# An output projection as four pairs in seven half-size products, with its weight sums made earlier in the kernel

## The chip, the cores and the metric

The kernel runs on one core of one Trainium2 chip. The time is device microseconds (us) of one launch. The kernel before was timed three times: 1026.96, 1028.63 and 1029.95 us, median 1028.63. One execution was also profiled; its own time was 1028.81 us. The engines have short names throughout: PE multiplies matrices (PEld is its weight load), DVE is the vector engine, ACT the scalar engine, POOL the GpSimd engine, SP the one that issues most transfers.

## The reference

One decoder layer on 512 tokens of 1024 channels, float32. Two mixers run on the normed input: gated linear recurrence (RG-LRU) and sparse attention with sixteen heads. They are merged by two gates, the merged result goes through an output projection back to the residual stream, and a gated feed-forward block with a short convolution follows.

```python
merged = sigmoid(h @ w_mgr) * (rnn @ w_ro) + sigmoid(h @ w_mga) * (att @ w_ao)
x = x + merged @ w_out                    # 1024 x 1024: what the change is about
h2 = rms_norm(x, g2)
u = causal_dwconv(h2 @ w_up)              # 1024 x 6144, in 24 pairs of column blocks
y = x + (gelu(u[:, :3072]) * u[:, 3072:]) @ w_down
```

(Names are shortened; the layer's remaining parts lie ahead of these lines.)

## The kernel before

Everything is kept transposed: 128 channels on the partitions, the 512 tokens along the free axis. A projection takes a block of 128 output channels, and for each of its eight input blocks k three products (`mm3`, lines 204 to 206): high half of the weight by high half of the input, high by low, low by high. So an output block costs 24 matmuls of 512 columns. The high half of a weight, `whi`, is a cast on ACT (line 167); the low half, `wlo`, is a subtraction on DVE (line 175), or under the attention heads on POOL, in four pieces (line 172). `whi` and `wlo` have three buffers each, the raw weight `wraw` two.

The stages in order: first norm and key compression; sixteen heads, between whose steps units of other projections ("fills", three matmuls each) are put by `FILL_RATE` and `FILL_MORE`; attention output and recurrence; the merge; the output projection `w_out`; the second norm with the first up-projection; the feed-forward block; the down-projection.

The merge runs a list of steps, `MERGE`. For each output block m, `roa` is 24 matmuls, `a` six, `b` two (line 1158). `rob` prepares weights that two blocks share. Behind `b`, DVE multiplies by the gate (1159), adds the attention part (1160), and the block is split into `mh` (ACT, line 229) and `ml` (DVE, line 230). `w_out` then takes eight blocks with `mm3`, adds the residual (1172), and prepares the second norm: `xh`, `xl`, the squares, and a chain that makes the tokens' scale factors (1184 to 1198).

The last 18 of the 24 feed-forward pairs are already in another form. A pair is two output blocks of 128 channels; with the inputs' eight blocks cut into two halves and the tokens into two halves, it is a 2 by 2 block product, and seven half-size products replace eight. Each is four k by three matmuls of 256 columns (`prod`, 1305 to 1307): 84 per pair. `seed` does four of the seven (weights u1 and u2) and combines them (1323 to 1327), `rest` does the other three (weights u3 and u4). Of a pair's weights three are sums of weights. `sums` makes these ahead of time in DRAM: SP writes the first terms (1214), then POOL issues three accumulating transfers in turn (1217), each of which must wait for the one before. When a set's steps are issued is told by `SUM_AT` and `SUM_RATE`, as a function of the position in the list of weights.

```python
if n < len(js): first(js[n], h)                      # SP, two halves
add(js[n - 1], slice(0, 64), a["wa"][js[n - 1]])      # POOL, then
add(js[n - 2], slice(96, 128), self.ws[js[n - 2]][32:64])
add(js[n - 3], slice(64, 96), self.ws[js[n - 3]][96:128])
```

In most stages the order on each engine comes from a scheduler with priorities; from the first up-projection on, PE's order is that of the code (`manual_schedule`).

## Time and profile before

| what | value |
|---|---|
| median of three runs | 1028.63 us |
| profiled execution: its time, its span | 1028.81 us, 1027.0 us |
| busy: PE, DVE, ACT, POOL | 1014.5, 750.3, 614.2, 250.7 us |
| heads (85 to 355 us): PE, DVE, POOL busy of 270.00 | 267.27, 223.43, 105.37 us |
| merge (545 to 605 us): PE, DVE busy of 60.00 | 59.21, 40.70 us |
| output projection (605.00 to 648.30): PE, DVE busy of 43.30 | 43.30, 22.40 us |
| feed-forward pairs in half-size products (715 to 892): PE busy | 37.64 of 38.00, then 139.00 of 139.00 us |

The span is the time between the first and the last instruction of one execution; the 1.81 us between it and the execution's time lie outside what the profile shows. A stage's own row tells more than the shares of the whole span: where PE's busy time is as long as the stretch, the stage ends when its matmuls are issued, and where it is shorter, the difference is PE's waiting.

### The profile page before, as it was taken

To read this page: it belongs to the slowest core of one execution; us is meant where nothing else is said; L and a number is where in the kernel's file an instruction comes from. 1 tells how busy PE (TensorE), PEld (TensorE's weight loads), DVE (VectorE), ACT (ScalarE), POOL (GpSimd) and SP (SyncE) were. 2 spreads that over 40 slices of the span, in tenths; PEclk is the share of its full clock that TensorE was granted. 3 is DMA by queue.
4 is the path that set the end of the run, shared out by engine and by line. 5 is a ranking of instruction groups with operands and counts; after the bars stand their busy time and mean duration, and the time that the engine had idled before them with its cause. 6 is when DMAs were issued, how large, how long until landed. Compare 5 with 4: busy or idle time off the path is not lost.

```text
span 1027.0 us, 15691 instructions
## 1 busy us (share of the span) xinstructions
PE 1014.5 (99%) x5657; PEld 881.5 (86%) x5657; DVE 750.3 (73%) x1441; ACT 614.2 (60%) x1034; POOL 250.7 (24%) x324
## 2 busy tenths in 40 slices
PE   8999999999999999999999999999999999999998
PEld 6888888988888888888887888888999999988886
DVE  6778879888878787679598564599798888933333
ACT  6466777877777663478788534365566656533320
POOL 0264435334433300332332014222211111100000
PEclk9999999999999999999999999999999999999999
DMA  7434443354535567865432977657876566632312
GB/s 235 87 112 112 134 119 108 106 137 108 157 101 158 127 223 202 232 190 171 146 92 85 294 230 204 179 149 213 259 204 201 176 196 187 202 99 88 102 62 82
DMA packets 63022, 160.88 MB, mean 157 GB/s; under 512 B 16283, under 2 KB 17691, under 8 KB 60064
## 3 DMA queue, kind: packets, MB, share of 16 engines
q1 hardware_dynamic: 56896, 137.92, 41.1%
q0 software_dynamic: 5904, 21.81, 12.4%
q8 instruction: 44, 0.72, 0.3%
q14 instruction: 34, 0.28, 0.1%
q10 hardware_dynamic: 144, 0.15, 0.1%
HBM read 150.63 MB, written 44.04 MB: 190 GB/s over the span
## 4 chain that ended last, share of the span: by engine, by line
PE 80%; DVE 11%; ACT 4%; issue 2%; DMA 2%; SPq 0%; DVEq 0%; ACTq 0%
PE mm L206 16%; PE mm L205 16%; PE mm L204 16%; PE mm L1307 5%; PE mm L1305 5%; PE mm L1306 5%; PE O L899 3%; PE T L908 3%; DMA wraw<-in_w 2%; PE S L868 1%; PE v L750 1%; PE S L869 1%; DVE wlo L175 1%; ACT s L879 1%; DVE s L872 1%
## 5 line engine op out<-in xcount | busy, mean ns | idle before, releaser
L167 ACT CAST whi<-wraw 128x1024 fp32r<-128x1024 f32 (+2 forms) x202 | 202.7, 1005 | 224.9 <-PE misc L205 77.0
L175 DVE TENSOR_TENSOR wlo<-wraw,whi 128x1024 fp32r<-128x1024 f32 (+1 forms) x167 | 193.4, 1159 | 134.6 <-ACT whi L167 134.4
L204 PE MATMUL mm<-xh,whi 128*128 128x512 f32 x456 | 178.7, 392 | 0.0
L206 PE MATMUL mm<-xh,wlo 128*128 128x512 f32 x456 | 178.5, 391 | 0.0
L205 PE MATMUL mm<-xl,whi 128*128 128x512 f32 x456 | 178.2, 391 | 0.0
L172 POOL TENSOR_TENSOR wlo<-wraw,whi 128x256 fp32r<-128x256 f32 (+2 forms) x139 | 101.5, 783 | 131.9 <-ACT whi L167 118.9
L206 PEld LDWEIGHTS mm<-xh,wlo 128*128 128x128 f32 x456 | 85.6, 188 | 18.5
L204 PEld LDWEIGHTS mm<-xh,whi 128*128 128x128 f32 x456 | 85.7, 188 | 16.8
L205 PEld LDWEIGHTS mm<-xl,whi 128*128 128x128 f32 x456 | 85.7, 188 | 16.6
L879 ACT ACTIVATE s<-s,bs,rq 128x128 f32<-128x128 f32 (+3 forms) x128 | 82.5, 647 | 17.2 <-DVE bs L876 17.1
L230 DVE TENSOR_TENSOR ptl<-T,pth 128x512 fp32r<-128x512 f32 x80 | 54.9, 687 | 16.6 <-ACT pth L229 15.7
L204 PE MATMUL mm<-fh,whi 128*128 128x512 f32 x168 | 65.4, 389 | 0.0
L205 PE MATMUL mm<-fl,whi 128*128 128x512 f32 x168 | 65.4, 389 | 0.0
L206 PE MATMUL mm<-fh,wlo 128*128 128x512 f32 x168 | 65.4, 389 | 0.0
L229 ACT CAST pth<-T 128x512 fp32r<-128x512 f32 x80 | 46.2, 581 | 28.7 <-PE T L908 28.0
L872 DVE CUSTOM_DVE_ANT_0 s<-S,cc 128x128 f32<-128x128 f32 (+3 forms) x128 | 58.3, 483 | 2.2 <-PE S L869 1.9
L1217 POOL DMA_DIRECT2D ws<-ws x36 | 28.5, 791 | 117.6 <-DMA ws<-ws 45.9
L908 PE MATMUL T<-cc,s 128*128 128x128 f32 x320 | 48.5, 273 | 1.6 <-DVE ptl L230 1.0
L908 PEld LDWEIGHTS T<-cc,s 128*128 128x128 f32 x320 | 39.3, 140 | 12.0 <-DVE ptl L230 2.0
L1249 DVE SCALAR_TENSOR_TENSOR y<-mm,pp,y 128x511 f32<-128x511 f32 (+1 forms) x60 | 44.2, 741 | 0.1
L899 PE MATMUL O<-pth,v 128*128 128x512 f32 (+3 forms) x128 | 42.8, 352 | 0.3 <-ACT hsq L645 0.3
L884 DVE TENSOR_SCALAR s<-s,sm 128x256 f32<-128x256 f32 (+3 forms) x106 | 40.9, 431 | 1.0
(393 smaller groups left out, 2642.5 us busy)
## 6 DMA issues: line engine op xcount, KB each, us to landing
wraw<-in_w SPq DMA_DIRECT2D x126, 512.0 KB, 3.5
ws<-in_wi SPq DMA_DIRECT2D x36, 512.0 KB, 5.1
wraw<-ws SPq DMA_DIRECT2D x72, 256.0 KB, 3.2
wraw<-in_w SPq DMA_DIRECT2D x54, 256.0 KB, 3.3
ws<-in_wa POOLq DMA_DIRECT2D x18, 512.0 KB, 6.0
ws<-ws POOLq DMA_DIRECT2D x36, 256.0 KB, 4.6
xr<-in_x SPq DMA_DIRECT2D x16, 256.0 KB, 4.9
x<-in_x SPq DMA_DIRECT2D x8, 256.0 KB, 4.5
```

The lines of the kernel that those rows point to most:

```text
L167: self.last_hi = nc.scalar.copy(hi[:, :n], raw[:, :n])
L172: nc.gpsimd.tensor_sub(lo[:, e], raw[:, e], hi[:, e].bitcast(F32))
L175: nc.vector.tensor_sub(lo[:, :e], raw[:, :e], hi[:, :e].bitcast(F32))
L204: nc.tensor.matmul(ps, wh, xh, start=first, stop=False)
L205: nc.tensor.matmul(ps, wh, xl, start=False, stop=False)
L206: nc.tensor.matmul(ps, wl, xh, start=False, stop=last)
L230: self.nc.vector.tensor_sub(lo, src, hi.bitcast(F32))
L872: nc.vector.tensor_tensor_reduce(s[i, x], ps[:, x - xs[0]], mask, 1.0, -3e38, ALU.add, ALU.max, mx[:, x, i:i + 1])
L879: self.last_exp = nc.scalar.activation(s[t, x], s[t, x], AF.Exp, bias=bs[:, x, t:t + 1], scale=rq[:, t], accum_out=sm[:, x, t:t + 1])
L899: nc.tensor.matmul(O[:, q0:S], lhsT, r, start=first[0], stop=(last and n == len(rhs) - 1))
L908: nc.tensor.transpose(T[:, off:off + 128], s[i, x][:, 128 * j:128 * j + 128], self.ident)
L1305: nc.tensor.matmul(ps, w[0][:, c], xh, start=start and k == 0, stop=False, skip_group_check=True)
```

## The change

The eight blocks of `w_out` become four pairs, numbered 24 to 27, in the form that the feed-forward pairs have. `prod`, `seed` and `rest` move from the feed-forward function to methods that both stages call. The operands that the seven products need (`b11`, `t1`, `t2`, `t3`, `t4`, `b21`, `b22`) are built in the merge, behind each `b` step, by a new `prep`. The merge takes its output blocks in the order `MP`, so that the two blocks of one operand follow each other, and its last block in two column halves. Four more sets of weight sums are made, and the schedule of the sums is new: 15 sets are issued under the heads instead of 8, and three instead of ten are left for the stages behind the merge. The operands lie in what was the room of the first norm's `xh` and `xl`; the second norm's get a room of their own (`x2`). One fill unit more stands at the sixth step of head 14 (`FILL_MORE`), and three k of the second up-projection are put ahead of the token-scale matmuls.

```diff
-FILL_MORE = {..., (12, 1): 2}
+FILL_MORE = {..., (12, 1): 2, (14, 5): 1}
-SUM_AT, SUM_RATE = 20, ((43, 1.0), (66, 2.4), (82, 16.0), (116, 2.0), (999, 3.0))
+SUM_AT, SUM_RATE = 20, ((43, 0.5), (66, 3.0), (82, 16.0), (105, 32.0), (117, 1.5), (999, 3.0))
-MERGE = ("roa0 roa1 roa2 rob0 a0 a1 roa3 b0 b1 roa4 rob1 a2 b2 roa5 a3 b3 roa6 rob2 a4 b4 a5 b5 roa7 rob3 "
-         "a6 b6 a7 b7").split()
+MERGE = ("roa0 roa1 roa2 rob0 a0 a1 roa3 b0 b1 roa4 rob1 a2 b2 a3 b3 roa5 rob2 a4 b4 a5 b5 roa6 rob3 a6 b6 "
+         "roa7 a7 b7").split()
+MP = [4 * (m % 2) + m // 2 for m in range(8)]
+WO = "s24 s25 r24 s26 r25 s27 r26 r27".split()
...
+        def prep(k, x1, x2):
+            lo, hi = slice(0, 256), slice(256, 512)
+            v = nc.vector
+            if x2 is None:
+                op("b11", k, x1[:, lo])
+                v.tensor_sub(x1[:, lo], x1[:, lo], x1[:, hi])
+                op("t1", k, x1[:, lo])
+                return
+            t2 = mr.tile([128, 256], F32, name="mt", bufs=1)
+            t34 = mr.tile([128, S], F32, name="mtt", bufs=1)
+            v.scalar_tensor_tensor(t2, x1[:, lo], -1.0, x2[:, hi], ALU.mult, ALU.subtract)
+            op("t2", k, t2)
+            v.tensor_sub(t34[:, lo], x2[:, hi], x1[:, hi])
+            v.scalar_tensor_tensor(t34[:, hi], t2, -1.0, x2[:, lo], ALU.mult, ALU.subtract)
+            op("t3", k, t34, True)
+            op("b21", k, x2, True)
...
-                nc.vector.tensor_mul(sg[m], ps[m], sg[m])
-                nc.vector.tensor_add(sg[m], sg[m], self.ma[:, m])
-                self.split(self.mh[:, m], self.ml[:, m], sg[m])
+                for t in (slice(0, S),) if m < 7 else (slice(256, 512), slice(0, 256)):
+                    nc.vector.tensor_mul(sg[m][:, t], ps[m][:, t], sg[m][:, t])
+                    nc.vector.tensor_add(sg[m][:, t], sg[m][:, t], self.ma[:, MP[m], t])
+                prep(m // 2, sg[m - m % 2], sg[m] if m % 2 else None)
...
-        for m in range(8):
-            wt = self.w("wo", m)
-            ps = self.ps.tile([128, S], F32, name="mm", bufs=self.mmb)
-            for k in range(KO):
-                self.mm3(ps, wt, slice(128 * k, 128 * k + 128), (self.mh[:, k], self.ml[:, k]), k == 0, k == KO - 1)
+            for step in WO:
+                j = int(step[1:])
+                if step[0] == "s":
+                    part[j] = self.seed(j, 3 if j == FC else 4)
+                else:
+                    rest(j, *part.pop(j))
...
+            w2 = self.w("u2", j)
+            self.prod(d, w2, 512, "t1")
+            for ks in (range(late), range(late, 4)):
+                self.prod(c, w, 512, "t2", True, ks)
+                self.prod(e, w2, 0, "t3", False, ks)
...
         ps = [self.proj("up", 0)]
+        g = self.proj_g("up", FC)
+        for _ in range(3):
+            next(g)
...
-        js = list(range(NPL, FC))
+        js = [*range(FC, FC + 4), *range(NPL, FC)]
```

The order on the engines changes at three places. In the rows below, "waits" names the semaphores that an instruction waits for, and "x3" is a count.

PE at the end of the merge, before: the last weight product, the two matmuls of `b7`, and the first three of `w_out`.

```order
L206 MATMUL mm<-hgh,wlo 128x512
L1158 MATMUL mm<-hgh,whi 128x512
L1158 MATMUL mm<-hgb,whi 128x512
L204 MATMUL mm<-mh,whi 128x512 [waits Activation_49]
L205 MATMUL mm<-ml,whi 128x512
L206 MATMUL mm<-mh,wlo 128x512 [waits DVE_49]
```

The same place after. `mxh` and `mxl` are the high and low halves of `b11`, `t1` and `t2`; `myh` and `myl`, below, those of the other four operands.

```order
L217 MATMUL mm<-hgh,wlo 128x512
L1210 MATMUL mm<-hgh,whi 128x512
L1210 MATMUL mm<-hgb,whi 128x512
L1277 MATMUL mm<-mxh,whi 128x256 [waits Activation_49]
L1278 MATMUL mm<-mxl,whi 128x256
L1279 MATMUL mm<-mxh,wlo 128x256 [waits DVE_49]
```

And where the first pair's `seed` ends, after:

```order
L1277 MATMUL mm<-myh,whi 128x256
L1278 MATMUL mm<-myl,whi 128x256
L1279 MATMUL mm<-myh,wlo 128x256
L1277 MATMUL mm<-mxh,whi 128x256 [waits Activation_49]
L1278 MATMUL mm<-mxl,whi 128x256 [waits DVE_49]
L1279 MATMUL mm<-mxh,wlo 128x256
L1277 MATMUL mm<-myh,whi 128x256 [waits Activation_49]
L1278 MATMUL mm<-myl,whi 128x256 [waits DVE_49]
L1279 MATMUL mm<-myh,wlo 128x256
```

The matmuls are half as wide, and the last six of the first `seed` (k = 3 of `t2` and `t3`) wait for operands of the merge's last block.

DVE at the same place, before: the merge's last two blocks (`sg` is the gate's tile, `ma` the attention part).

```order
L1159 TENSOR_TENSOR sg<-mm,sg 128x512 [waits PE_49]
L1160 TENSOR_TENSOR sg<-sg,ma 128x512 [waits DVE_49]
L1159 TENSOR_TENSOR sg<-mm,sg 128x512 [waits PE_49]
L230 TENSOR_TENSOR ml<-sg,mh 128x512 [waits Activation_49]
L1160 TENSOR_TENSOR sg<-sg,ma 128x512 [waits DVE_49]
L175 TENSOR_TENSOR wlo<-wraw,whi 128x1024 [waits DMAHW1_49,Activation_49]
L230 TENSOR_TENSOR ml<-sg,mh 128x512 [waits Activation_49]
L1172 TENSOR_TENSOR xn<-mm,xr 128x512 [waits DMAHW4_49,PE_49]
```

After: from the second-last weight of the merge's end to the last operand. `mt` is `t2`; `mtt` holds `t3` and `t4`.

```order
L186 TENSOR_TENSOR wlo<-wraw,whi 128x1024 [waits DMAHW0_49,DMAHW1_49,PE_49,Activation_49]
L1213 TENSOR_TENSOR sg<-mm,sg 128x256 [waits PE_49]
L1213 TENSOR_TENSOR sg<-mm,sg 128x256
L1214 TENSOR_TENSOR sg<-sg,ma 128x256 [waits DVE_49]
L186 TENSOR_TENSOR wlo<-wraw,whi 128x1024 [waits Activation_49]
L1214 TENSOR_TENSOR sg<-sg,ma 128x256 [waits DVE_49]
L1175 SCALAR_TENSOR_TENSOR mt<-sg 128x256 [waits DVE_49]
L1177 TENSOR_TENSOR mtt<-sg 128x256
L1178 SCALAR_TENSOR_TENSOR mtt<-mt,sg 128x256 [waits DVE_49]
L241 TENSOR_TENSOR myl<-sg,myh 128x2x256 [waits Activation_49]
L241 TENSOR_TENSOR mxl<-mt,mxh 128x256 [waits Activation_49]
L241 TENSOR_TENSOR myl<-mtt,myh 128x2x256 [waits Activation_49]
```

The last block's multiplication now comes in halves, and three subtractions and three low halves stand behind it, with a weight's low half between them.

DVE behind the merge's first two blocks, before: `wlo` 128x512 is the low half of the weights of `rob1`, which the step `a2` needs.

```order
L1159 TENSOR_TENSOR sg<-mm,sg 128x512 [waits DMASW5_49,PE_49,Activation_49]
L1159 TENSOR_TENSOR sg<-mm,sg 128x512 [waits PE_49,Activation_49]
L181 TENSOR_TENSOR whi<-wraw,whi 84x2x128 [waits DMAHW1_49,Activation_49]
L1160 TENSOR_TENSOR sg<-sg,ma 128x512 [waits DVE_49] x2
L175 TENSOR_TENSOR wlo<-wraw,whi 128x512
L230 TENSOR_TENSOR ml<-sg,mh 128x512 [waits DMASW7_49,DMASW0_49,Activation_49]
L230 TENSOR_TENSOR ml<-sg,mh 128x512 [waits Activation_49]
L175 TENSOR_TENSOR wlo<-wraw,whi 128x1024 [waits DMAHW3_49,Activation_49]
```

After:

```order
L1213 TENSOR_TENSOR sg<-mm,sg 128x512 [waits DMASW2_49,PE_49,Activation_49]
L1213 TENSOR_TENSOR sg<-mm,sg 128x512 [waits PE_49,Activation_49]
L192 TENSOR_TENSOR whi<-wraw,whi 84x2x128 [waits DMAHW7_49,Activation_49]
L1214 TENSOR_TENSOR sg<-sg,ma 128x512 [waits DVE_49] x2
L241 TENSOR_TENSOR mxl<-sg,mxh 128x256 [waits Activation_49]
L1177 TENSOR_TENSOR mtt<-sg 128x256 [waits DMASW5_49,DMASW6_49,DMASW4_49,DVE_49]
L1169 TENSOR_TENSOR sg<-sg 128x256 [waits DVE_49]
L241 TENSOR_TENSOR myl<-sg,myh 128x2x256 [waits Activation_49]
L241 TENSOR_TENSOR mxl<-sg,mxh 128x256 [waits Activation_49]
L1175 SCALAR_TENSOR_TENSOR mt<-sg 128x256
L186 TENSOR_TENSOR wlo<-wraw,whi 128x512
L1178 SCALAR_TENSOR_TENSOR mtt<-mt,sg 128x256 [waits DVE_49]
```

Six operations of the operands of block pair 0 and 1 now stand ahead of that `wlo`.

POOL under the heads, before. `ws_1338` and the like are the sets of sums in DRAM; a `wlo` of 128x256 is a quarter of a weight.

```order
L1217 DMA ws_1338<-ws_1338 32x2048 [waits DMAHW1_49,DMASW0_49]
L1217 DMA ws_1338<-ws_1338 32x2048 [waits DMASW1_49]
L172 TENSOR_TENSOR wlo<-wraw,whi 128x256 [waits DMAHW0_49,PE_49,Activation_49]
L172 TENSOR_TENSOR wlo<-wraw,whi 128x256 x3
L1217 DMA ws_1779<-in_wa 64x2048 [waits DMAHW4_49]
L172 TENSOR_TENSOR wlo<-wraw,whi 128x256 [waits DMAHW2_49,PE_49,Activation_49]
L172 TENSOR_TENSOR wlo<-wraw,whi 128x256 x3
L172 TENSOR_TENSOR wlo<-wraw,whi 128x256 [waits DMAHW3_49,PE_49,Activation_49]
L172 TENSOR_TENSOR wlo<-wraw,whi 128x256 x3
```

After:

```order
L1334 DMA ws_1338<-ws_1338 32x2048 [waits DMAHW1_49,DMASW0_49]
L1334 DMA ws_1616<-in_wa 64x2048 [waits DMAHW3_49]
L1334 DMA ws_1338<-ws_1338 32x2048 [waits DMASW1_49]
L183 TENSOR_TENSOR wlo<-wraw,whi 128x256 [waits DMAHW0_49,PE_49,Activation_49]
L183 TENSOR_TENSOR wlo<-wraw,whi 128x256 x3
L1334 DMA ws_1616<-ws_1616 32x2048 [waits DMAHW4_49,DMASW2_49]
L1334 DMA ws_1616<-ws_1616 32x2048 [waits DMASW4_49]
L1334 DMA ws_1783<-in_wa 64x2048 [waits DMAHW6_49]
L183 TENSOR_TENSOR wlo<-wraw,whi 128x256 [waits DMAHW2_49,PE_49,Activation_49]
L183 TENSOR_TENSOR wlo<-wraw,whi 128x256 x3
L183 TENSOR_TENSOR wlo<-wraw,whi 128x256 [waits DMAHW5_49,PE_49,Activation_49]
L183 TENSOR_TENSOR wlo<-wraw,whi 128x256 x3
```

In the same stretch of the queue two sets begin where there was one, and their transfers stand between the weights' low halves.

## Rows read from the trace of the kernel before

**Rows 1.** The page, parts 1 and 2: busy times; PE's granted clock in 40 slices.

```profile
PE 1014.5 (99%) x5657; PEld 881.5 (86%) x5657; DVE 750.3 (73%) x1441; ACT 614.2 (60%) x1034; POOL 250.7 (24%) x324
...
PEclk9999999999999999999999999999999999999999
```

**Rows 2.** Busy time by stretch: stretch, length, PE, PEld, DVE, ACT, POOL, PEclk, DMA share, GB/s.

```profile
85.00:355.00 270.00, 267.27 (x1544) 230.61 (x1543) 223.43 (x683) 203.15 (x466) 105.37 (x141) 1.00 0.47 124
545.00:605.00 60.00, 59.21 (x261) 48.69 (x260) 40.70 (x53) 35.42 (x47) 9.06 (x10) 1.00 0.66 202
605.00:648.30 43.30, 43.30 (x193) 35.83 (x192) 22.40 (x28) 17.58 (x24) 14.48 (x11) 1.00 0.75 213
753.00:892.00 139.00, 139.00 (x1194) 139.00 (x1193) 118.89 (x174) 87.95 (x114) 18.17 (x14) 1.00 0.62 193
```

**Rows 3.** Timeline of PE, output projection's first matmul and the one behind its last (start, length).

```profile
604.85 0.40 PE L204 MATMUL mm<-mh,whi 128*128 128x512 f32 x1
...
648.40 0.39 PE L204 MATMUL mm<-xh,whi 128*128 128x512 f32 x1
```

**Rows 4.** Timeline of PE, half-size products: first, first of the next pair, behind the last.

```profile
715.12 0.28 PE L1305 MATMUL mm<-b11h,whi 128*128 128x256 f32 x1
...
720.73 0.28 PE L1305 MATMUL mm<-b11h,whi 128*128 128x256 f32 x1
...
892.16 0.40 PE L204 MATMUL mm<-fh,whi 128*128 128x512 f32 x1
```

**Rows 5.** Timeline of DVE in the half-size products: starts of operations that stand back to back.

```profile
732.10 1.22 DVE L175 TENSOR_TENSOR wlo<-wraw,whi 128x1024 fp32r<-128x1024 f32 x1
733.23 0.74 DVE L1249 SCALAR_TENSOR_TENSOR y<-mm,pp,y 128x510 f32<-128x510 f32 x1
733.89 0.74 DVE L1249 SCALAR_TENSOR_TENSOR y<-mm,npw,y 128x511 f32<-128x511 f32 x1
...
736.86 0.43 DVE L1325 TENSOR_TENSOR mm<-mm,ac 128x256 f32<-128x256 f32 x1
737.20 0.42 DVE L1326 TENSOR_TENSOR mm<-mm,ac 128x256 f32<-128x256 f32 x1
```

**Rows 6.** Timeline of DVE and PE at the merge's step a2.

```profile
574.54 1.28 DVE L1160 TENSOR_TENSOR sg<-sg,ma 128x512 f32<-128x512 f32 x2
575.75 0.68 DVE L175 TENSOR_TENSOR wlo<-wraw,whi 128x512 fp32r<-128x512 f32 x1
...
578.11 0.39 PE L206 MATMUL mm<-hgh,wlo 126*128 126x512 f32 x1
```

**Rows 7.** Waits of POOL in the heads, 85 to 357 us: total, times, longest.

```profile
POOL wlo L172 <- ACT whi L167: 66.6, 15, 14.3
POOL ws L1217 <- PE T L908: 22.8, 5, 5.9
POOL ws L1217 <- DMA ws<-ws: 20.7, 8, 4.4
POOL ws L1217 <- DMA ws<-in_wi: 18.0, 6, 6.0
POOL ws L1217 <- DMA ws<-in_wa: 5.8, 1, 5.8
```

**Rows 8.** Timeline of the heads: a DVE operation beside POOL, and a wait of PE.

```profile
344.62 3.06 POOL L172 TENSOR_TENSOR wlo<-wraw,whi 128x256 fp32r<-128x256 f32 x4
...
345.20 2.51 DVE L876 SCALAR_TENSOR_TENSOR bs<-mx,rq 128x4 f32<-128x4 f32 x1
...
354.41 0.66 PE L908 MATMUL T<-cc,s 128*128 128x128 f32 x4 [1.02 <-DVE ptl L230]
```

**Rows 9.** Groups by form: POOL's low halves and issues of the sums.

```profile
L172 POOL TENSOR_TENSOR wlo<-wraw,whi 128x256 fp32r<-128x256 f32 x136 | 100.2, 790 | 131.9 <-ACT whi L167 118.9 <-PE T L908 9.4 <-PE sp L681 3.7
L1217 POOL DMA_DIRECT2D ws<-ws x36 | 28.5, 791 | 117.6 <-DMA ws<-ws 45.9 <-DMA ws<-in_wi 41.4 <-DMA ws<-in_wa 17.9
```

**Rows 10.** Waits of PE, 715 to 753 us.

```profile
PE mm L1307 <- DVE wlo L175: 0.4, 1, 0.4
```

More of the change, by code (lines that the diff above doesn't have):

```diff
@@ L318, in build @@
                     self.attn_out()
-            with tp("hgp", side="right") as self.hgp:
+            X2 = ExitStack()
+            with X2, ExitStack() as HG:
+                self.hgp = HG.enter_context(tp("hgp", side="right"))
                 self.hgh, self.hgl = {}, {}
@@ L1145, in merge @@
         for step in MERGE:
+            if step == "roa5":
+                self.wpri = HPRI
             kind, m = step[:-1], int(step[-1])
@@ L1200, in w_out, with prod, seed, rest @@
         self.up0 = ps
+    def prod(self, ps, w, o, name, start=False, ks=range(4)):
+        nc = self.nc
+        for k in ks:
+            c = slice(o + 128 * k, o + 128 * k + 128)
+            xh, xl = (x[:, k] for x in self.SB[name])
+            nc.tensor.matmul(ps, w[0][:, c], xh, start=start and k == 0, stop=False, skip_group_check=True)
+            nc.tensor.matmul(ps, w[0][:, c], xl, start=False, stop=False, skip_group_check=True)
+            nc.tensor.matmul(ps, w[1][:, c], xh, start=False, stop=(k == 3), skip_group_check=True)
+    def seed(self, j, late=4):
+        nc = self.nc
+        r0 = self.ps.tile([128, S], F32, name="mm", bufs=self.mmb)
+        r1 = self.ps.tile([128, S], F32, name="mm", bufs=self.mmb)
+        a, d, c, e = r0[:, 0:256], r0[:, 256:512], r1[:, 0:256], r1[:, 256:512]
+        w = self.w("u1", j, WLEAD)
+        self.prod(a, w, 0, "b11", True)
+        if late == 4:
+            self.prod(c, w, 512, "t2", True)
+            w = self.w("u2", j, WLEAD)
+            self.prod(d, w, 512, "t1")
+            self.prod(e, w, 0, "t3")
+        else:
+            w2 = self.w("u2", j)
[3 more added lines that the diff above has]
+                self.prod(e, w2, 0, "t3", False, ks)
+        with self.tc.high_priority(HPRI):
+            ad = self.sd.tile([128, S], F32, name="ad", bufs=2)
+            ac = self.sd.tile([128, 256], F32, name="ac", bufs=2)
+            nc.scalar.copy(ad, r0)
+            nc.vector.tensor_tensor(ac, c, ad[:, 0:256], ALU.add)
+            nc.vector.tensor_tensor(d, d, ac, ALU.add)
+            nc.vector.tensor_tensor(c, e, ac, ALU.add)
+            self.last_sum = nc.vector.tensor_tensor(e, c, ad[:, 256:512], ALU.add)
+        return r0, r1
+    def rest(self, j, r0, r1):
+        w = self.w("u3", j, WLEAD)
+        self.prod(r0[:, 256:512], w, 0, "b22")
+        self.prod(r0[:, 0:256], w, 512, "b21")
+        w = self.w("u4", j, 1 if j == FC + 3 else WLEAD)
+        self.prod(r1[:, 0:256], w, 0, "t4")
     def sums(self):
```

146 lines of the change are left out of this document (75 added, 71 removed).

## The prediction

> **What bounds the kernel now.** I read the page's busy times first: PE is busy 1014.5 of 1027.0 us, DVE 750.3, at a granted clock that shows 9 in all forty slices [rows 1]. A reader should conclude two things: time comes off only where PE has less to do, and an addition on another engine costs only where PE then waits. So I read stretch by stretch [rows 2]. In the output projection PE is busy 43.30 of 43.30 us and DVE 22.40: a stage whose length is its matmuls. In the merge PE is busy 59.21 of 60.00 and DVE 40.70. In the half-size products PE is busy 139.00 of 139.00 and PEld as long: there the weight loads run without a gap. In the heads PE is busy 267.27 of 270.00.
>
> **The output projection.** Removed: 8 blocks by 24 matmuls of 512 columns, 192, from 604.85 to 648.40 [rows 3]: 43.55 us, or 0.2268 each. (The 0.39 us of one row is its length in the pipeline; the step from start to start is what counts.) Added: 4 pairs by 84, 336 matmuls of 256 columns. Their step is read from the same operation in the feed-forward block: 48 of them from 715.12 to 720.73, 0.1169; all 1512 from 715.12 to 892.16 [rows 4], 177.04 us less the 0.4 us that PE waited there [rows 10], 0.1168. So 336 by 0.1168 is 39.24 us, and **PE's part is -4.3 us**. It can't come out much below: the step barely changed over 1512 matmuls.
>
> A half-width matmul does not cost half: 0.1168 is over half of 0.2268, which is why seven eighths of the work saves 4.3 and not 5.4 us. The Trainium skill (TensorE: Matmul & The Clock Gate, "LDWEIGHTS (loading the stationary operand)") sets a weight load at columns divided by 1.2, in ns; for 128 columns that makes 107 ns, and 336 of them 35.8 us, a saving of 7.7. PEld's full busy time agrees that the load sets the pace, but the measured step is 117, and the measurement decides.
>
> **Does DVE keep up in that stage?** Back to back, DVE starts a 1024-wide operation's successor after 1.13 us, a 512-wide one's after 0.66, a 256-wide one's after 0.34 [rows 5]; their listed lengths (1.22, 0.74, 0.43) overlap. A pair needs three low halves of 1024 (3.4) and one of 512 (0.66), four 256-wide sums (1.4), two residual additions and two low halves of the second norm (2.6): 8.1 us, by lengths 9.1, and PE takes 9.8. It fits either way, without much room. The weights of later pairs are cast when a buffer comes free and so are made about 1 us ahead of use. I take nothing.
>
> **Seed 24, the first four products.** Count from the end of the last `b7` matmul. PE needs the low half of k = 3 of `t2` after 43 matmuls, 5.0 us, and of `t3` 0.35 us later. The order on DVE from there is one weight, two half multiplications, an addition, a weight, an addition, `t2`, `t3`, `t4`, and low halves of b21 and b22, `t2`, and `t3` and `t4`. The first weight's buffer is free eight matmuls (1.8 us) before zero; with its cast it ends at 0.5. Then two by 0.34, 0.34, 1.13, 0.34, 0.46 and 0.34 and 0.46 (a successor that needs the result waits for the full length), 0.66, 0.34: the low half of `t2` at 5.3, of `t3` and `t4` at 5.95. PE loses 0.3 and then 0.3: **+0.6 us**. By lengths instead of steps the chain ends at 6.6: +1.3. If the scheduler's instructions overlap better it is 0.
>
> **The merge.** Per pair of blocks DVE loses two 512-wide low halves (1.3) and gains about 3.6 us of subtractions and halves: 2.3 by four is 9 us more on 40.70 of 60.00 [rows 2]. It fits, so only the order matters. At `a2` the weight's low half came right behind the additions, 575.75 to 576.43; PE first used it at 578.11 [rows 6], 1.7 us of cover. Now five 256-wide operations and one 512-wide stand ahead of it: 5 by 0.34 and 0.66, 2.4 us, so it ends at 578.8: **+0.7 us** (by lengths 1.2; nothing if PE is already late there). At `a4` and `a6` the low half stands ahead of the operands' operations; nothing.
>
> **The token scales and the first up-projection.** The 24 matmuls of the first block and three k of the second now stand ahead of the scale chain's matmuls, so POOL's sum of squares has 2 us more; on DVE no weight stands in the chain any more. Nothing, and nothing of it was PE's wait before.
>
> **The heads.** The added unit of fills is three matmuls that otherwise run later; it is worth something only where PE waits, and it stands near the 1.02 us wait at 354.41 [rows 8]. Between 0 and 0.7; I take **-0.3**. The sums: seven more sets, three issues of 0.79 us each [rows 9] and their waits, in front of POOL's low halves. I take 0, because POOL waited 66.6 us for ACT's high halves in this stretch [rows 7], time in which it had nothing due; this is the term I trust least (the third rival).
>
> **Feed-forward.** Three sets instead of ten remain behind the merge. PE waited 0.4 us between 715 and 753 [rows 10]; **-0.1**, between 0 and -0.4.
>
> **The sum** is -4.3 + 0.6 + 0.7 - 0.3 - 0.1 = -3.4. The profiled execution took 1028.81 us, its span 1027.0, with 1.81 outside, which I leave as it is; that execution lies 0.18 above the median 1028.63. So the median becomes **1025.2 us**. Some 0.3% (3.1 us) is what a measurement of this kernel can tell from no change, so the bound of faster is 1025.5.
>
> **Rivals.**
> *The stalls don't come.* The operations on DVE overlap as the rows show at best, `a2` and seed 24 cost nothing, the added fill covers 0.7 and the feed-forward wait goes: -4.3 - 0.7 - 0.4 = -5.4, 1023.2. For it: the two waits of the first seed are 0.3 us each, within the error of such a chain. Against: the order at `a2` is fixed, and 2.4 us does not fit into 1.7.
> *DVE is late through the merge and the first pairs.* Steps of 0.34 hold only where an operation doesn't need the one before; many here do, or wait for ACT's cast between. Then the lengths count: 1.2 at `a2`, 1.3 at seed 24, and where the pair's 9.1 of 9.8 us runs over by two waits for ACT, some 0.5 per pair: -4.3 + 1.2 + 1.3 + 1.5 - 0.3 = -0.6, 1028.0. For it: DVE's busy time was already two thirds of the merge. Against: in the half-size products DVE is busy 118.89 of 139.00 us [rows 2], beside an unbroken PE.
> *POOL becomes late under the heads, and the kernel is slower.* One set cost POOL three issues (2.4 us) and, over eight sets, 22.8 + 20.7 + 18.0 + 5.8 = 67 us of waiting [rows 7], 8.4 each. Seven more at this price are 76 us, and the time in which POOL waited for work was 66.6. From the point where a weight's low half ends after PE's first use of it, every further microsecond is PE's: 76 less 66.6 is 9, so 1025.2 + 9 = 1034. For it: two sets begin where one did. Against: much of the waiting was POOL being early for a transfer, and shrinks when POOL comes later; by issues and one transfer's wait of 4.4 a set costs 7, and seven make 48 of 66.6. A wait of DVE adds to it: `bs`, a four-element operation, took 2.51 us beside POOL's 3.06 [rows 8].
>
> On that last row the Trainium skill (SBUF — State Buffer, "SBUF: two separate sides") has a rule that speaks against this change: a DVE operation with two SBUF inputs and a GpSimd operation that reads SBUF exclude each other for their whole length. The row agrees with it (2.51 within POOL's 3.06). By it a low half that POOL makes later only moves such a block, so it adds no sum of its own; the third rival holds it.
>
> **Chances.** The forecast 0.47, with its own range 1024.2 to 1026.5; no stalls 0.19; DVE late 0.19; POOL late 0.15. Faster holds all of the second and some two thirds of the first (0.31): 0.50. Slower is the last, 0.15. Same is the rest, 0.35. The range runs from the second case to beyond the third: 1022.6 to 1029.5, leaving out the fourth.
>
> **What would show it.** Right: the stretch from `b7` to the up-projection's first matmul takes 39.2 to 40.2 us, its half-size matmuls step by 0.117, PE waits some 0.7 us for a weight's low half at `a2`, and twice for low halves of operands in the first seed; PE's idle time in the heads is no more than the 2.7 us of before. Wrong: PE waiting for POOL's low halves in the heads (third rival), or for `myl`, `mxl` or `wlo` in more than one pair of the output projection (second), or a stage that starts late because the sums of pairs 24 to 27 weren't in DRAM.

## The result and the profile after

The changed kernel takes 1041.11 us (median of four runs, 1038.47 to 1043.52); before took 1028.71 beside it. The ratio is 1.0126, interval [1.0105, 1.0148]: slower by 12.4 us, where 1025.2 had been forecast. Its profiled execution took 1038.47 us with a span of 1036.7, that is 9.7 over the span of before.

The page's busy times after (they answer to [rows 1]):

```profile
PE 1017.2 (98%) x5801; PEld 888.6 (86%) x5801; DVE 781.1 (75%) x1495; ACT 628.4 (61%) x1058; POOL 260.3 (25%) x336
```

PE is busy 2.7 us longer, though it has 4.3 us less to do in one stage. To see where, I took the first matmul of each stage from PE's timeline, in both kernels and in most of the runs below; the next one's start ends a stage. These are lengths in us, of the one profiled execution of each kernel.

| kernel | start | heads | attention output, recurrence | merge | output projection | first up-projection | plain pairs | half-size pairs |
|---|---|---|---|---|---|---|---|---|
| before | 85.5 | 282.6 | 177.6 | 59.1 | 43.5 | 11.8 | 54.9 | 177.0 |
| after | 82.7 | 290.5 | 179.1 | 60.2 | 39.9 | 16.4 | 54.9 | 178.4 |
| e1 old rate | 83.6 | 285.6 | 177.8 | 60.0 | 42.1 | 17.6 | 54.9 | 178.7 |
| e2 additions first | 83.2 | 295.5 | 179.3 | 60.3 | 40.1 | 14.3 | 54.9 | 178.8 |
| e3 both | 84.8 | 282.9 | 177.6 | 59.1 | 41.2 | 20.0 | 54.9 | 180.7 |
| e4 before, new rate | 82.8 | 290.3 | 177.6 | 59.2 | 43.5 | 11.8 | 54.9 | 176.4 |
| e5 short squares | 83.7 | 295.4 | 178.5 | 60.3 | 39.9 | 12.0 | 54.9 | 177.5 |
| e8 squares on DVE | 82.5 | 285.6 | 177.7 | 58.7 | 43.7 | 14.3 | 54.9 | 178.9 |
| e9 sets in the recurrence | 84.4 | 284.6 | 186.9 | 59.3 | 40.6 | 12.2 | 54.9 | 177.3 |
| e13 more copies (before) | 83.0 | 284.1 | 177.5 | 59.2 | 43.5 | 11.8 | 54.9 | 176.4 |
| e15 sets in the pairs | 86.6 | 282.6 | 179.4 | 58.1 | 40.8 | 12.4 | 54.9 | 192.5 |
| e16 no chain (before) | 83.1 | 282.8 | 177.6 | 59.2 | 43.6 | 11.8 | 54.9 | 176.4 |
| e17 apart | 82.8 | 282.5 | 192.3 | 61.0 | 39.9 | 16.4 | 54.9 | 181.2 |
| e19 spread | 82.7 | 284.9 | 178.1 | 58.7 | 40.4 | 14.7 | 54.9 | 183.7 |

The start differs between executions of one program as well (the kernels of e4, e13 and e16 have the unchanged start and show 82.8 to 83.1), so its -2.8 is not the change's. The rest: heads +7.9, up-projection +4.5, recurrence +1.6, half-size pairs +1.4, merge +1.1, output projection -3.7.

The heads differ between executions too. In e2 and e5 all four engines have the same instructions there, in the same order, as in the changed kernel, and the heads take 295.5 and 295.4 us, not 290.5; e1, e3 and e8, with one schedule, show 285.6, 282.9 and 285.6. So the length of the heads in one profile is good to some 5 us, and a cause of their loss has to rest on medians of several executions as well. The four times of the changed kernel lie in two groups (1038.47 and 1038.89; 1043.32 and 1043.52), and the profile is of the shorter one: of the 12.4 us of the medians it shows 9.7. What the longer two lost was not profiled.

The same stages of after by engine (columns as in [rows 2]):

```profile
85.00:355.00 270.00, 263.52 (x1507) 226.44 (x1506) 223.27 (x666) 196.42 (x453) 120.22 (x159) 0.99 0.69 177
612.50:652.40 39.90, 39.76 (x337) 39.53 (x336) 36.94 (x55) 25.05 (x35) 6.24 (x4) 1.00 0.58 192
652.40:668.70 16.30, 13.93 (x58) 10.91 (x57) 9.59 (x16) 5.20 (x8) 5.68 (x4) 0.90 0.30 97
```

In the heads PE is idle 6.5 of 270.00 us (2.7 before) and POOL busy 15 us more. In the output projection PE has no gap worth the name, and the 11.8 us up to the plain pairs have become 16.4 (the row's 16.3) at a mean granted clock of 0.90.

The output projection's first matmul and the up-projection's (they answer to [rows 3]):

```profile
612.52 0.29 PE L1277 MATMUL mm<-mxh,whi 128*128 128x256 f32 x1
...
652.40 0.39 PE L215 MATMUL mm<-xh,whi 128*128 128x512 f32 x1
```

652.40 less 612.52 is 39.88 us, against 43.55.

### The profile page after: what moved, and what is told of

Read it like the earlier page. It is cut to its first block, busy times and chain, and to the rows that moved or that the text cites. A ratio compares the mean times of both kernels' runs of the same rounds, so it can differ in the third digit from the quotient of the medians.

```text
span 1036.7 us, 16130 instructions
## 1 busy us (share of the span) xinstructions
PE 1017.2 (98%) x5801; PEld 888.6 (86%) x5801; DVE 781.1 (75%) x1495; ACT 628.4 (61%) x1058; POOL 260.3 (25%) x336
## 4 chain that ended last, share of the span: by engine, by line
PE 73%; DVE 11%; ACT 6%; DMA 4%; issue 3%; POOL 2%; SPq 1%; POOLq 0%; DVEq 0%; ACTq 0%
PE mm L217 13%; PE mm L216 13%; PE mm L215 13%; PE mm L1277 7%; PE mm L1279 7%; PE mm L1278 7%; PE O L913 2%; PE T L922 2%; ACT s L893 2%; DMA ws<-in_wi 1%; POOL wlo L183 1%; PE v L764 1%; DVE ptl L241 1%; ACT whi L178 1%; PE S L882 1%
## 5 line engine op out<-in xcount | busy, mean ns | idle before, releaser
L178 ACT CAST whi<-wraw 128x1024 fp32r<-128x1024 f32 (+2 forms) x210 | 209.4, 999 | 200.4 <-PE misc L216 77.0
L186 DVE TENSOR_TENSOR wlo<-wraw,whi 128x1024 fp32r<-128x1024 f32 (+1 forms) x175 | 202.0, 1156 | 130.5 <-ACT whi L178 130.2
L216 PEld LDWEIGHTS mm<-xl,whi 128*128 128x128 f32 x456 | 86.2, 189 | 17.6 <-DVE xl L261 0.6
L893 ACT ACTIVATE s<-s,bs,rq 128x128 f32<-128x128 f32 (+3 forms) x128 | 82.5, 648 | 22.9 <-DVE bs L890 22.9
L1375 POOL TENSOR_TENSOR f<-y 128x512 f32<-128x512 f32 x24 | 36.3, 1514 | 162.4 <-DVE y L1366 161.1
L1334 POOL DMA_DIRECT2D ws<-ws x44 | 35.0, 795 | 164.3 <-DMA ws<-ws 63.6
L241 DVE TENSOR_TENSOR ptl<-T,pth 128x512 fp32r<-128x512 f32 x80 | 54.9, 688 | 18.0 <-ACT pth L240 17.3
```

Source lines behind the costliest of these rows:

```text
L178: self.last_hi = nc.scalar.copy(hi[:, :n], raw[:, :n])
L186: nc.vector.tensor_sub(lo[:, :e], raw[:, :e], hi[:, :e].bitcast(F32))
L216: nc.tensor.matmul(ps, wh, xl, start=False, stop=False)
L241: self.nc.vector.tensor_sub(lo, src, hi.bitcast(F32))
L893: self.last_exp = nc.scalar.activation(s[t, x], s[t, x], AF.Exp, bias=bs[:, x, t:t + 1], scale=rq[:, t], accum_out=sm[:, x, t:t + 1])
```

## What the lines of the three losses show

**Heads.** POOL's waits after, in the window of [rows 7]:

```profile
POOL ws L1334 <- DMA ws<-ws: 42.9, 13, 6.0
POOL ws L1334 <- DMA ws<-in_wa: 33.9, 6, 7.8
POOL ws L1334 <- DMA ws<-in_wi: 30.0, 11, 5.4
POOL wlo L183 <- ACT whi L178: 16.9, 11, 2.5
POOL ws L1334 <- PE S L883: 10.7, 2, 7.6
```

Its waits in front of the sets' issues went from 73 us (the 67 of [rows 7], and 6.0 that the same view puts down to a matmul of `S`) to 118 (42.9, 33.9, 30.0 and 10.7), and the time in which it waited for a weight's high half, its slack, from 66.6 to 16.9. In this execution most of what that does to PE is seen at one place. POOL, ACT and PE there:

```profile
296.82 0.78 POOL L1334 DMA_DIRECT2D ws<-ws  x1 [7.61 <-PE S L883]
...
301.22 0.78 POOL L1334 DMA_DIRECT2D ws<-ws  x1 [0.80 <-DMA ws<-ws]
305.42 0.80 POOL L1334 DMA_DIRECT2D ws<-in_wa  x1 [3.42 <-DMA ws<-in_wi]
305.96 1.03 POOL L183 TENSOR_TENSOR wlo<-wraw,whi 128x256 fp32r<-128x256 f32 x1
306.66 1.33 POOL L831 TENSOR_TENSOR cs<-cs,cmx 128x512 f32<-128x512 f32 x1
307.67 1.00 POOL L183 TENSOR_TENSOR wlo<-wraw,whi 128x256 fp32r<-128x256 f32 x1
308.37 1.30 POOL L832 TENSOR_TENSOR cs<-cs,rqt 128x512 f32<-128x512 f32 x1
...
309.71 0.63 ACT L833 ACTIVATE cs<-cs 128x512 f32<-128x512 f32 x1 [4.05 <-POOL cs L832]
...
312.55 0.67 PE L922 MATMUL T<-cc,s 128*128 128x128 f32 x2 [3.48 <-DVE ptl L241]
```

`cs` is a step of the heads' own compressed scores. POOL waits three times, with one weight's quarters between: 7.61 us in front of a set's second accumulation (the view names a matmul; at the same place of e4, below, it names the set's first accumulation), 0.80 for the third, and 3.42 for SP's first terms of the next set. Then it alternates a weight's quarters with the two `cs` operations, which end at 309.7. ACT waits 4.05 us for them with the heads' casts queued behind, DVE makes the last operand after these, and PE waits 3.48 us, in a stage where it had waited 2.7 in all. Behind that wait the granted clock was 0.50 (columns as in [rows 2]):

```profile
314.00:316.00 2.00, 2.00 (x7) 1.71 (x6) 2.00 (x8) 0.27 (x1) 2.00 (x4) 0.50 0.40 148
```

It stayed so from 312.6 to 316.0, which is 1.7 us of PE's work lost. All of PE's waits in the heads went from 2.7 to 7.4 us; with the 1.7 that is 6.4 of the 7.9, and the rest is not assigned.

**Up-projection.** DVE, then POOL, then PE, at the end of the output projection:

```profile
651.78 0.68 DVE L1227 TENSOR_TENSOR xn<-xr,mm 128x512 f32<-128x512 f32 x1
652.54 1.57 DVE L186 TENSOR_TENSOR wlo<-wraw,whi 128x1024 fp32r<-128x1024 f32 x1
654.03 1.77 DVE L261 SCALAR_TENSOR_TENSOR xl<-xn,pp,xh 128x512 fp32r<-128x512 f32 x1
655.73 2.30 DVE L186 TENSOR_TENSOR wlo<-wraw,whi 128x1024 fp32r<-128x1024 f32 x1
657.96 0.67 DVE L1227 TENSOR_TENSOR xn<-xr,mm 128x512 f32<-128x512 f32 x1
...
651.19 5.76 POOL L272 TENSOR_TENSOR sqa<-sqa,sq 128x512 f32<-128x512 f32 x3 [7.32 <-ACT sq L271]
...
656.96 0.39 PE L217 MATMUL mm<-xh,wlo 128*128 128x512 f32 x1
659.44 0.51 PE L215 MATMUL mm<-xh,whi 128*128 128x512 f32 x1 [2.09 <-ACT xh L260]
...
660.80 0.63 PE L215 MATMUL mm<-xh,whi 128*128 128x512 f32 x1
661.23 0.63 PE L216 MATMUL mm<-xl,whi 128*128 128x512 f32 x1
```

`xn` is the residual addition, `xl` the second norm's low half, `sqa` the sum of squares. Beside POOL's three additions (651.19 to 656.95) a weight's low half takes 2.30 us and `xl` 1.77 (1.22 and 0.74 elsewhere); `xn`, which reads PSUM, keeps 0.68 (at 651.78; the one at 657.96 comes after the additions). The eighth block's `xn` so starts at 657.96, and PE waits 2.09 us for its `xh`. Behind the wait the matmuls step by 0.43 us instead of 0.2268: the granted clock fell to the lower of its two levels, 1.2 GHz, after PE had stood still, and PE ran so from 660.8 to 664.2, which costs another 1.7 us.

In the kernel before, `xl` and POOL's additions met as well, but there `xl` began just before each addition: it took 0.74 to 0.75 us and the addition 1.76 to 1.84, against 1.28 at 660.05 in the kernel after, where DVE was all but idle. So it was POOL that came late there, and PE waited for nothing.

**Merge.** The wait at `a2` and the one in the first seed:

```profile
585.62 0.50 PE L217 MATMUL mm<-hgh,wlo 126*128 126x512 f32 x1 [0.75 <-DVE wlo L186]
...
617.84 0.28 PE L1277 MATMUL mm<-myh,whi 128*128 128x256 f32 x1
618.26 0.39 PE L1278 MATMUL mm<-myl,whi 128*128 128x256 f32 x1
618.49 0.28 PE L1279 MATMUL mm<-myh,wlo 128*128 128x256 f32 x1
```

0.75 us at `a2` (the 0.8 us that PE waits for the low half at `a0` stands in the kernel before too); and from 617.84 to 618.26 one step of 0.42 instead of 0.117, which with the next one (0.23) is the seed's late operand: 0.4 us or so in one place.

## Experiments

**e4: the new schedule alone, on the kernel before.**

```diff
-SUM_AT, SUM_RATE = 20, ((43, 1.0), (66, 2.4), (82, 16.0), (116, 2.0), (999, 3.0))
+SUM_AT, SUM_RATE = 20, ((43, 0.5), (66, 3.0), (82, 16.0), (105, 32.0), (117, 1.5), (999, 3.0))
```

> The kernel before with only the new schedule of the sums (18 sets, 15 of them under the heads); no other part of the change. Theory: it alone costs the heads some 7 us: 1035 to 1037 us. Rival: the schedule is harmless and the heads' loss comes from the other moves (the added fill, another order of the attention output's weights): within 2 us of 1028.7.

1035.27 us, ratio 1.0080 [1.0063, 1.0097]; the heads take 290.3 us, as in the changed kernel, with one wait of PE of 3.91 us at the same place. So the schedule of the sums costs nearly 8 us by itself, and no other part of the change is needed for it.

**e13: the bytes without POOL.**

```diff
             nc.sync.dma_start(self.ws[j][o], a["wi"][j, o])
+            if j < NPL + 8:
+                for r in range(2):
+                    x = self.drp.tile([64, 2048], F32, name=f"wx{j}_{h}_{r}")
+                    nc.sync.dma_start(x, a["wi"][j, o])
```

> The kernel before, with SP's first transfer of each of the eight sets under the heads issued three times instead of once (the two others to DRAM that nothing reads): about the bytes of seven more sets, without an instruction on POOL. Theory: it is POOL's queue that costs the heads, not the bytes: 1027.7 to 1029.5 us, PE's waits in the heads as before. Rival: the added transfers delay weights and the sets' chains by themselves: 1033 us or more, as with the new schedule (1035.3).

1028.12 us, ratio 1.0003 [0.9990, 1.0015]. The heads take 284.1 us. Plain transfers of that size on SP's queue are not the cost.

**e16: the sets without their chain.** e4's kernel; the second and third accumulation add a part of the input, so the sums lack the terms that the set's own partial sums would have brought.

```diff
-add(js[n - 2], slice(96, 128), self.ws[js[n - 2]][32:64])
-add(js[n - 3], slice(64, 96), self.ws[js[n - 3]][96:128])
+add(js[n - 2], slice(96, 128), a["wa"][js[n - 2]][0:32])
+add(js[n - 3], slice(64, 96), a["wa"][js[n - 3]][32:64])
```

> The kernel before with the new schedule of the sums (as in the run that took 1035.3 us), but the second and third accumulation of each set add a part of the input instead of the set's own partial sum, so that POOL's issue of one no longer waits for the one before (the sums of weights are left wrong by it); as many issues, as many bytes. Theory: POOL's blocked waits are what costs the heads: 1028.5 us (1027 to 1030.5), PE's waits in the heads as in the kernel before. Rival: the issues' own 0.8 us each and the moves of the low halves cost it: 1033 to 1036.

1026.96 us, ratio 0.9985 [0.9973, 0.9998]; heads 282.8. With as many issues on POOL the loss is gone. It isn't the sum of POOL's waiting that counts, though:

```profile
POOL ws L1217 <- DMA ws<-in_wi: 76.0, 20, 6.7
POOL wlo L172 <- ACT whi L167: 26.5, 12, 5.5
```

The first of these and the smaller waits in front of issues make 104 us here too. What is gone are the waits in a row, for a transfer that POOL itself had issued just before. The same place in e4, then in e16:

```profile
294.94 0.78 POOL L1217 DMA_DIRECT2D ws<-ws  x1 [6.72 <-DMA ws<-in_wa]
...
305.83 1.33 POOL L817 TENSOR_TENSOR cs<-cs,cmx 128x512 f32<-128x512 f32 x1
...
297.28 0.79 POOL L1217 DMA_DIRECT2D ws<-in_wa  x1 [5.67 <-DMA ws<-in_wi]
...
300.54 1.16 POOL L817 TENSOR_TENSOR cs<-cs,cmx 128x512 f32<-128x512 f32 x1
```

POOL still waits 5.67 us for SP's terms there, but the wait ends at 297.28, and `cs` starts 5 us earlier.

**e17: the full sets, the accumulations apart.** Each is queued behind the low half of a later weight, and waits for what was issued two sets ago; the schedule's last rate is 2.0 instead of 3.0.

```diff
-            if 0 <= n - 1 < len(js):            # and n - 2, n - 3
+            if 0 <= n - 2 < len(js):            # and n - 4, n - 6
...
-            nc.gpsimd.dma_start(self.ws[j][o], src, accum_op=ALU.add, max_dma_last_dim=8192)
+            with self.tc.issue_after(self.last_lo.ins) if self.pool_lo else nullcontext():
+                nc.gpsimd.dma_start(self.ws[j][o], src, accum_op=ALU.add, max_dma_last_dim=8192)
```

> The changed kernel with its sets under the heads, but a set's three accumulations apart in POOL's queue (each behind the low half of a later weight, two sets' distance instead of one), so that what each waits for has long landed; the sums are complete, and the last ones are made at a little closer spacing. Theory: blocked issues were the heads' cost; the heads take 283 us instead of 290 and the kernel 1033 us (1031.5 to 1035), what remains being the up-projection's late last block and the merge. Rival: the other work in POOL's queue moves with the accumulations and makes new waits in the heads or the recurrence: 1037 or more.

The heads take 282.5 us, as forecast: sixteen sets begun there, most of them finished, cost nothing when no accumulation follows its predecessor directly. But the kernel takes 1046.36 us, ratio 1.0184 [1.0152, 1.0216]. The last sets bunch where the heads end, and PE waits once, for 11.63 us, in the attention output:

```profile
388.38 0.80 PE L217 MATMUL mm<-oh,wlo 128*128 128x512 f32 x1 [11.63 <-DVE wlo L186]
```

In the kernel of e18, which shares this, the transfer engines are full there (columns as in [rows 2]):

```profile
345.00:375.00 30.00, 30.00 (x153) 25.32 (x153) 16.86 (x33) 16.69 (x33) 14.57 (x20) 1.00 1.01 262
375.00:385.00 10.00, 3.80 (x17) 2.81 (x15) 4.04 (x7) 4.38 (x7) 0.77 (x1) 0.91 1.05 332
```

There DVE waits 9.5 us for a gate's tile that SP loads, and the low half that PE needs stands behind that on DVE.

**e10: the heads' own steps off POOL.** Three operations on `cs` and `cl` per key group go to DVE, the schedule stays.

```diff
-        nc.gpsimd.tensor_tensor(s3, s3, b16(m), ALU.subtract)
+        nc.vector.tensor_tensor(s3, s3, b16(m), ALU.subtract)
```

(and likewise the multiplication behind it, and that of `cl`).

> The changed kernel, its 15 sets under the heads kept, with three operations of each key group's compressed scores (two on cs, one on cl) on DVE instead of POOL. Theory: what was late in the heads was cs, behind a blocked issue of a sum and a weight's pieces in POOL's queue; ACT waited 4 us for it with the heads' own casts queued behind, and PE 3.5 us. Off POOL, that wait of PE goes and the heads lose 4 to 5 us less: 1036.5 us (1035 to 1038). Rival: PE waits because the weights' low halves or the transfers are late as such; then the heads lose as much as before, and DVE's twelve more operations add to it: 1041 or more.

1040.28 us, ratio 1.0134 [1.0098, 1.0170]: inconclusive to wrong. The wait of 3.5 us is gone, but PE now waits 1.6, 1.4 and 1.0 us for maxima that DVE makes late; the heads take 291.9. So that `cs` alone carries the loss to PE is read from the rows above and not shown by this run.

**e1: the changed kernel with the schedule of before** (the line of e4 the other way round).

> The changed kernel with the schedule of the sums of before (8 sets under the heads instead of 15; the four new sets still come first). Theory: the heads lost some 8 us because POOL, blocked by the added sets, comes late to the heads' own steps; they come back, and the kernel takes about 1033 us (1031 to 1035), with the heads' waits of PE back to some 3 us. Rival: the loss sits in the merge and the output projection, and the schedule matters only where the sets are needed; then 1039 to 1042, and if the sets left for the feed-forward block now collide there, more.

1036.90 us, ratio 1.0094 [1.0079, 1.0109]; heads 285.6. Neither the theory nor the rival had this time. Some 4 us came back, not 8: the heads gain 4.9 (no more than they differ between executions), but sets now stand in the merge and the output projection (42.1 instead of 39.9).

**e2: the last residual additions first on DVE.**

```diff
-                f(self.xn[:, m], xr, r)
+                with self.tc.high_priority(2 * HPRI if j == FC + 3 else 0):
+                    f(self.xn[:, m], xr, r)
```

> The changed kernel with only the last pair's two residual additions put ahead in the scheduler's priority on DVE. Theory: the first up-projection lost 4.5 us because its eighth input block came 2.1 us late, behind two low halves of weights on DVE, and the matmuls behind the wait then ran at a lower granted clock; with the addition one weight earlier the wait goes or shrinks below 0.5 us and the kernel takes 1036.5 us (1035 to 1038). Rival: the lateness comes from DVE's operations being stretched beside POOL's sums of squares (a low half took 2.30 instead of 1.22 us), whichever comes first; then the wait stays above 1 us and the time within 2 us of 1041.

1042.36 us, ratio 1.0147 [1.0131, 1.0163]: the rival. The addition comes earlier, but `xl` behind it is stretched, and PE waits 2.2 us for that. The stage itself takes 14.3 us, not 16.4, for the most part because the granted clock stayed at 1.00 behind this wait; the heads of this profile are the longer ones.

**e5: short squares.** POOL's seven additions of squares work on one column, so the squares of the other 511 are left out of the sum.

```diff
-            nc.gpsimd.tensor_tensor(self.sqa, self.sqa, sq, ALU.add)
+            c = slice(0, 1 if pool is getattr(self, 'mr', None) else S)
+            nc.gpsimd.tensor_tensor(self.sqa[:, c], self.sqa[:, c], sq[:, c], ALU.add)
```

> The changed kernel in which POOL's seven additions of the second norm's squares work on one column instead of 512 (the squares of the other columns are left out of the sum). Theory: DVE's operations with two operands in SBUF wait for POOL's additions there (a weight's low half took 2.30 instead of 1.22 us, xl 1.77 instead of 0.74, while the residual addition, with one operand in PSUM, kept its 0.68); with short additions they take 1.2 and 0.75 again, PE's wait for the eighth block falls from 2.1 us to below 0.5, the lower clock behind it goes, and the time is 1037 us (1035.5 to 1038.5). Rival: DVE is simply full there, and the order holds the last block back; then the lengths or the wait stay, and the time stays within 2 us of 1041.

1034.15 us, ratio 1.0053 [1.0032, 1.0074], and the stage takes 12.0 us, not 16.4. DVE at the same place:

```profile
657.58 1.23 DVE L186 TENSOR_TENSOR wlo<-wraw,whi 128x1024 fp32r<-128x1024 f32 x1
658.72 0.75 DVE L261 SCALAR_TENSOR_TENSOR xl<-xn,pp,xh 128x512 fp32r<-128x512 f32 x1
659.38 1.22 DVE L186 TENSOR_TENSOR wlo<-wraw,whi 128x1024 fp32r<-128x1024 f32 x1
660.52 0.68 DVE L1228 TENSOR_TENSOR xn<-xr,mm 128x512 f32<-128x512 f32 x1
661.99 0.75 DVE L261 SCALAR_TENSOR_TENSOR xl<-xn,pp,xh 128x512 fp32r<-128x512 f32 x1 [0.79 <-ACT xh L260]
```

The low half takes 1.23 and 1.22 us again, `xl` 0.75, and PE waits for neither. (The median fell by 7, more than this stage's 4.4; the profiled execution, 1038.47, is the longest of four and has heads of 295.4, so only the stage is compared here.)

**e3 and e8: the edits together.** e3 is e1 with e2's edit and the low half of `rob` put first on DVE; e8 adds the last two squares to DVE.

```diff
+                with self.tc.high_priority(HPRI if name == "rob" else 0):
+                    nc.vector.tensor_sub(lo[:, :e], raw[:, :e], hi[:, :e].bitcast(F32))
...
-            self.norm_sq(m, self.xn[:, m], mr)
+            self.norm_sq(m, self.xn[:, m], mr, nc.vector if m > 5 else None)
```

> Both edits, and the low half of the two blocks' shared weight put first on DVE in the merge. Theory: the three losses are independent and add up: 1033 less 4.5 less 0.7, so about 1028 us (1026 to 1030); against before that is no change or a small gain. Rival: what is taken off in one place is waited for in the next, and the time stays above 1033.

> The kernel of the run with both edits, with the last two additions of squares on DVE, behind the last xl, instead of on POOL. Theory: PE's waits there (0.3 and 2.9 us) and the slower matmuls behind them (some 2 us) go; 1035.3 less 5 is 1030.3 us (1029 to 1032). Rival: the wait only moves to the chain of the token scales, as DVE has two operations of 0.66 more in front of it; then 1033 to 1035.5.

1035.33 us, ratio 1.0074 [1.0058, 1.0091], and 1031.62 us, ratio 1.0036 [1.0023, 1.0049]. e3's theory failed (1028 expected): `xl` still met POOL's squares, PE waited 2.9 us, and the lower clock around that wait cost some 5 more, so the stage took 20.0. e8 takes 3.7 off; its output projection is at 43.7 again, with PE waiting for late weights (0.8 and 1.0 us), where sets now stand; e3, with the same schedule, had 41.2 there, and why they differ is open.

**e9, e11, e12, e15, e18, e19: another place for the sets.** All are e8 with another schedule (e18: e17's way); from e12 on, six of the eight input blocks of both first up-projection blocks come ahead of the last two on PE.

```diff
+e9:  20, ((43, 1.0), (75, 1.3), (105, 32.0), (117, 1.5), (999, 3.0))
+e11: 10, ((43, 1.0), (66, 2.4), (105, 32.0), (117, 1.5), (999, 2.4))
+e15: 20, ((43, 1.0), (76, 2.4), (105, 32.0), (117, 1.0), (999, 1.4))
+e19: 20, ((43, 1.0), (67, 2.4), (70, 34.0), (117, 1.2), (999, 2.3))
...
+        g0, g = self.proj_g("up", 0), self.proj_g("up", FC)
+        for x in (g0,) * 6 + (g,) * 3:
+            next(x)
```

> The kernel of the run before this one, with eight sets under the heads, eight under the attention output and the recurrence, and six left behind. Theory: fourteen sets behind the merge made transfers and weights late in the feed-forward block (PE waited 2.5 us there in three places); with six left these waits go, and the recurrence, where PE never waited, hides the others: 1030.3 less 2.5 is 1027.8 us (1026 to 1029.5). Rival: POOL's transfers of the recurrence's conv and scan stand behind the blocked sums and PE then waits there: 1031 or more.

1035.96 us, 1.0078 [1.0058, 1.0098]: the rival. PE waits 4.57 us for a transfer of the recurrence that shares POOL's queue:

```profile
442.23 1.22 PE L1077 MATMUL mm<-st,whi 126*128 126x512 f32 x2 [4.57 <-DMA st<-xcl]
...
443.67 0.63 PE L217 MATMUL mm<-xl,whi 128*128 128x512 f32 x1
444.10 0.63 PE L218 MATMUL mm<-xh,wlo 128*128 128x512 f32 x1
```

> The kernel with both edits and the last squares on DVE, with the sums begun ten weights earlier: some eleven sets before the heads' end at the spacing of before, three in the recurrence, none in the merge and the output projection, eight behind. Theory: sets cost only where they stand close in POOL's queue or beside full stages; the output projection's late weights (0.8 and 1.0 us) and part of the feed-forward block's waits go, the heads stay as they were: 1029 us (1027.5 to 1031). Rival: more sets ahead of the heads' end cost there what is won behind: 1031 to 1034.

1041.61 us, 1.0132 [1.0109, 1.0154]: the start takes 92.9 us, and the pairs 184.7, with PE waiting for late low halves of weights. The output projection is down to 41.0 and the up-projection to 12.2.

> The same, and PE's order at the first up-projection changed: six of eight input blocks of both output blocks first, the seventh and eighth of both last. Theory: the last two input blocks then have some 4 us more before PE needs them, so its waits for xl (0.9 and 0.8 us in the run with the squares on DVE) and the slower matmuls behind them go: 2 to 3 us less than the run beside it, 1026.5 us (1025 to 1028). Rival: the chain of the token scales becomes the wait, since fewer matmuls stand between its start and its use: no more than 0.5 us less.

1042.47 us, 1.0150 [1.0128, 1.0173]: nothing gained, since without sets there e11 had no wait for `xl` left.

> The kernel with the interleaved up-projection, the sums begun as before (eight sets under the heads), four under the attention output and the recurrence, none in the merge and the output projection, the other ten close together from the plain feed-forward pairs on. Theory: the start and the heads cost what they cost before, the output projection and the up-projection run without the waits (in the run with the sums begun earlier PE waited 0.4 us there in all), and the sets come early enough for the last pairs: 1026.5 us (1025 to 1028.5). Rival: ten sets close together delay weights in the feed-forward block: 1029 or more.

1044.06 us, 1.0151 [1.0131, 1.0171]. All stages up to the plain pairs but the recurrence (179.4, with a wait of 1.3 for a transfer) are as forecast; the half-size pairs take 192.5 us with full transfer engines:

```profile
715.00:760.00 45.00, 40.94 (x328) 40.44 (x327) 30.97 (x45) 23.57 (x33) 10.14 (x10) 0.92 0.94 288
760.00:800.00 40.00, 34.41 (x267) 33.00 (x266) 30.83 (x39) 19.65 (x27) 11.21 (x12) 0.96 0.98 304
```

> The same with all the other edits (the residual additions and the shared weight's low half ahead on DVE, the last squares on DVE, the up-projection's two blocks interleaved). Stage by stage from earlier runs: heads 283 (282.6 before), merge 58.1 (59.15), output projection 40 (43.55), first up-projection 12.4 (11.84), feed-forward pairs 177 to 178.5 (177.04). Theory: the gains of these stages add up, 1025.5 us (1024 to 1027.5), faster than before by some 3. Rival: sets in the feed-forward block or the recurrence take it back: 1028 or more.

1043.61 us, 1.0161 [1.0129, 1.0193], for e17's reason.

> All edits but the accumulations apart, and the sums' schedule changed once more: eight sets under the heads and three behind them as in the kernel before, none in the merge, five near the plain feed-forward pairs, the rest with more room between them than in the run that took 1044 us. Stage by stage from earlier runs: heads 282.6 to 285, recurrence 177.6 (before 177.55), merge 58.1, output projection 40.7, first up-projection 12.4, feed-forward pairs 178 to 180. Theory: the feed-forward block was held back there by transfers alone (DMA share 0.94 to 0.98), and with room between the sets it isn't: 1027.5 us (1026 to 1030). Rival: eleven sets behind the merge can't be made beside the pairs' own weights in any order: 1032 or more.

1036.52 us, 1.0085 [1.0070, 1.0100]: the pairs still take 183.7 us, with eight short waits for a weight's low half (3.6 us in all).

No version that does the whole work beat the kernel before. The stages' best lengths were never met in one kernel.

## Why the prediction was wrong

- **The output projection** came out as worked out: 39.88 us measured, 39.24 plus 0.6 predicted. DVE kept up, busy 36.94 of 39.90 us. The first seed cost 0.4 us in one place instead of 0.3 in two, and the other steps are 0.1175 instead of 0.1168, 0.2 us in all: two small misses that cancel.
- **The merge**: 0.7 predicted at `a2`, 0.75 measured. Right. The stage grew by 1.1; the other 0.3 is not assigned.
- **The heads** are the step that failed first. It read: "I take 0, because POOL waited 66.6 us for ACT's high halves in this stretch". The measured loss is 7.9 us in the profile; e4 shows 7.7 of it by the schedule alone, and e13, e16 and e17 show the cause: not bytes and not issues, but an accumulation that waits for the one just issued. The third rival had the direction; that its 9 us came near is luck, as it looked at the wrong victim, the weights' low halves, and counted seven more sets. The trace begins sixteen under the heads against eight, eight more, and by the rival's own price that makes 86 less 66.6, 20 us. I counted POOL's slack as one sum over 270 us, and asked only who waits for the weights. POOL's queue also carries a step of the heads that ACT, DVE and PE wait for in turn, and there a few waits in a row are enough (read from the rows; e10 did not confirm it). The 0.3 us for the added fill can't be told in this.
- **The token scales and the first up-projection**: "Nothing, and nothing of it was PE's wait before." Measured 4.5 us: 2.4 of PE's waits, 1.7 of lower clock, the rest not assigned. The sentence looked at the scale chain only; the last residual addition, ahead of it, stands behind two weights on DVE, and I had priced DVE by lengths of a stage without asking what POOL did beside them. The Trainium skill's rule on the shared port pair (SBUF — State Buffer, "SBUF: two separate sides") was cited and then given no sum. The trace agrees with it in detail: two operands in SBUF, 2.30 and 1.77 us beside POOL's additions, 1.23 and 0.75 without them (e5); one operand in PSUM, 0.68 in both.
- **The feed-forward block**: -0.1 predicted, +1.4 measured (last section); PE waited 0.4 us there after as before. By the trace the sets that begin behind the merge went from five to three, not from ten to three, so there was less to gain. The attention output's +1.5, a wait for a weight's low half, was not in the sum; neither e4 (the schedule alone) nor e1 (the change with the old schedule) has it, so it takes both, and its cause stays open.

The range left out the case that came nearest: 0.15 was given to it, and its 1034 was still 7 us short.
